# Gathering experts' rows for 144 instead of 128 tokens, and dense products over 368 tokens instead of 384

## The chip, the core and the metric

The kernel runs on one core of one Trainium2 chip. The engines that matter here: TensorE (PE) does the matrix products, VectorE (DVE) and ScalarE (ACT) the elementwise work, GpSimd (POOL) some elementwise work and the issue of indirect DMAs, SyncE (SP) the issue of the weight loads. The metric is device time in microseconds (us), lower is better: the median of several runs of the whole program, which is one launch.

## What is computed

Two transformer blocks in float32, one after the other, on 512 tokens of width 1024 (the second block adds 16 meta tokens). The change touches one layer of the first block, a mixture of 16384 experts, each of them one row of `peer_u` and one row of `peer_v`. Each token picks 16 experts in each of 8 heads:

```python
def peer_ffn(h, w_pq, subkeys, u, v):
    ...
    fin_s, fin_pos = lax.top_k(cand_s, PEER_TOPK)
    expert_idx = jnp.take_along_axis(cand_i, fin_pos, axis=-1)
    gates = jax.nn.softmax(fin_s, axis=-1).astype(h.dtype)
    ...
        u_sel = jnp.take(u, ec, axis=0)
        act = jax.nn.gelu(jnp.einsum('chkd,cd->chk', u_sel, hc), approximate=False) * gc
        v_sel = jnp.take(v, ec, axis=0)
        return jnp.einsum('chk,chkd->cd', act, v_sel)
```

So a token's result is a sum of 128 rows of `v`, each weighted by a gate and by the GELU of a dot product of the token with a row of `u`. The rest of both blocks (convolutions, attention, retention, feed-forward layers) is the same before and after.

## The kernel before

**Two ways through the expert layer.** The last `ND = S - NS` = 384 tokens go the dense way: all 16384 experts are evaluated with matrix products, and a gate matrix that is zero nearly everywhere does the choosing. The first `NS` = 128 tokens go the gathered way, one token per partition: a "row step" fetches for each of the 128 partitions one row of `u` (or of `v`) by an indirect DMA of 512 KB, and VectorE multiplies and sums it. 128 row steps with `u` and then 128 with `v` make up the gathered part (class `_Gathered`; `read` issues the DMA on GpSimd's queue, `step` does VectorE's work and writes the read for two steps later; the tile `row` has `NROW = 4` buffers, so this read waits for the buffer of the step two before).

**The dense way.** Weights come in blocks of 1 MB. Each block is split into a rounded part `whi` (ScalarE, line 95) and a remainder `wlo` (line 96, VectorE in this layer), and each product is three passes: `whi` with both parts of the input and `wlo` with one. A block is 2 column groups x 8 slices of the contraction x 3 passes = 48 matmuls of 128x384 (`mm`, line 184). Experts are taken in 16 groups. A `u` group is 4 `u` blocks (`u_block`: product, GELU, tile `a`), a `v` group 4 `v` blocks that add into `X` (line 1133).

- First stretch: the `u` blocks of the first 12 groups, 48 blocks. Their activations `a` are spilled to DRAM (`ad`). Meanwhile the choice of experts runs on VectorE, and for each dense token two one-hot matrices are made by GpSimd, VectorE and ScalarE (`four`, four tokens at a time) and multiplied on TensorE (`gather`, line 1058) to the gate matrix, which goes to DRAM (`gd`).
- Second stretch: 80 blocks in the order u12, v12, v0, v1, v2, u13, v13, v3, v4, v5, and so on to v11. For a spilled group its gates (`g`, 1.5 MB) and activations (`a`, four pieces of 384 KB) are reloaded on GpSimd's queue during the `v` group ahead of it (`reload`, `back`), multiplied and split on VectorE and ScalarE (`weigh`, lines 1096 and 272 to 274). The tile `g8` has one buffer and `a` three, so the fourth piece of `a` waits until the first has been used. 12 `v` groups have such a reload in them; three (v2, v5, v8) are followed by a `u` group instead, and the last has neither reload nor row steps.

**What sets the order.** Everything that is not a dense product is put on a list `bg` with a cost by hand. After each slice of a product (3 matmuls) `step` adds `rate * t / 512` to a budget and takes items from the list while the budget is positive:

```python
        self.bg_left += self.rate * share
        while self.bg and self.bg_left > 0:
            cost, fn = self.bg.pop(0)
            self.bg_left -= cost
            fn()
```

A row step costs 1.3, a `weigh` 2.1. `EARLY` says how many row steps are woven into each third of the first stretch; `PACE` how many are put on the list per block in the second: `PACE[0]` in a `u` block, `PACE[1]` in a `v` block of a group with a reload (one more at its first block), `PACE[2]` in one of the three groups without. The list sets the order in which instructions are written; each engine then runs its own in that order, and waits for the others by semaphores. Whatever is left on the list at the end of the first stretch is written out at once (`flush`), as are the row steps left at the end (`finish`).

Of the kernel before, what the change touches and what calls it, by code (L numbers as in the profile page):

```python
# [18 lines left out]
P = 128  # L19
D = 1024  # L20
S = 512
NM = 16
T2 = S + NM
KT = D // P
# [6 lines left out]
NS = 128  # L31
ND = S - NS
TCH = 16
# [3 lines left out]
EARLY = (30, 30, 38)  # L37
PACE = (2.4, 1.45, 3.4)
# [756 lines left out]
class _Gathered:  # L795


    def __init__(self, K, tp, H):
        self.K, self.tp, self.H = K, tp, H
# [3 lines left out]
    def rows_of_h(self):  # L803

        nc = self.K.nc
        box = self.K.tp.tile([P, T2], F32, name="acc", tag="acc", bufs=1)
        self.gate, self.dots, self.index = box[:, :P], box[:, P:2 * P], box[:, 2 * P:3 * P].bitcast(U32)
        o = self.K.ps.tile([P, 1024], F32, name="mm", tag="mm", bufs=3)
        for k in range(KT):
            for i in range(2):  # L810
                nc.tensor.matmul(o[:, k * P:(k + 1) * P], self.H[i][:, k, :NS].bitcast(F32), self.K.ident, start=i == 0, stop=i == 1)
        nc.scalar.activation(self.h, o, AF.Copy)

    def begin(self, i, j):
        self.K.nc.vector.scalar_tensor_tensor(self.index, i, float(P), j, op0=OP.mult, op1=OP.add)  # L815
        for _ in range(NROW - 2):
            self.read()

    def read(self):
        n = self.nread  # L820
        if n == 2 * P:
            return
        t = self.tp.tile([P, D], F32, name="row", tag="row", bufs=NROW)
        src = self.K.d["u_rows"] if n < P else self.K.d["v_rows"]
        self.K.nc.gpsimd.indirect_dma_start(out=t, out_offset=None, in_=src,  # L825
                                            in_offset=bass.IndirectOffsetOnAxis(ap=self.index[:, n % P:n % P + 1], axis=0))
        self.rows[n] = t
        self.nread += 1

    def step(self):  # L830
        n, nc = self.ndone, self.K.nc
        s = n % P
        self.ndone += 1
        t = self.rows.pop(n)
        if n < P:
            nc.vector.tensor_tensor_reduce(t, t, self.h, 1.0, 0.0, OP.mult, OP.add, self.dots[:, s:s + 1])  # L836
            if s == P - 1:
                nc.scalar.activation(self.dots, self.dots, AF.Gelu)
                nc.vector.tensor_mul(self.dots, self.dots, self.gate)
        elif s == 0:  # L840
            self.sum = self.tp.tile([P, D], F32, name="sum", tag="hrow")
            nc.vector.tensor_scalar(self.sum, t, self.dots[:, :1], None, op0=OP.mult)
        else:
            nc.vector.scalar_tensor_tensor(self.sum, t, self.dots[:, s:s + 1], self.sum, op0=OP.mult, op1=OP.add)  # L844
        self.read()

# [11 lines left out]
    def more(self, n):  # L858
        self.due += n
        while self.due >= 1 and self.planned < 2 * P:  # L860
            self.K.bg.append((1.3, self.step))
            self.planned += 1
            self.due -= 1

    def finish(self, X):
        K, nc = self.K, self.K.nc
        self.more(2 * P)
        K.flush()
        for i in range(2):
            a = K.aux().rearrange("p (k t) -> p k t", k=4)  # L870
            for k in range(4):
                nc.tensor.transpose(a[:, k], self.sum[:, (4 * i + k) * P:(4 * i + k + 1) * P], K.ident)
            x = X[:, 4 * i:4 * i + 4, :NS]
            nc.vector.tensor_add(x, x, a)


def _peer(K, XA, X, nx):
# [5 lines left out]
    with tc.tile_pool(name="peer", bufs=1) as tp:  # L883
        H = nx.H
        HR = [x[:, :, NS:] for x in H]
        rest = _Gathered(K, tp, H)
# [10 lines left out]
        with tc.tile_pool(name="route", bufs=1) as rp:  # L897
# [78 lines left out]
            def small(name, dt=F32, tag=None):  # L976
                return rp.tile([P, HD * 16], dt, name=name, tag=tag or name, bufs=1)

            def gates(t):
                f = box["v"]  # L980
                v = rest.gate.rearrange("p (h k) -> p h k", h=HD) if t == 0 else rp.tile([P, HD, 16], F32, name="ge", bufs=1)
# [40 lines left out]
            def turn(t):  # L1022
                a = K.aux()
                for n, x in enumerate((box[0], box[1], box["v"].rearrange("p h k -> p (h k)"))):
                    nc.tensor.transpose(a[:, n * P:(n + 1) * P], x, K.ident)
                for n in range(3):
                    nc.vector.tensor_copy(IT[n][:, t * P - NS:(t + 1) * P - NS], a[:, n * P:(n + 1) * P])
                nc.vector.tensor_scalar(IT[3][:, t * P - NS:(t + 1) * P - NS], a[:, :P], -1.0, None, op0=OP.mult)

# [38 lines left out]
            for t in range(1, 4):  # L1068
                K.bg.append((1.8, lambda t=t: turn(t)))
                fours = [(1.1, lambda tb=tb, q=q: four(tb, q))  # L1070
                         for tb in range((t * P - NS) // TCH, ((t + 1) * P - NS) // TCH) for q in range(TCH // 4)]
# [4 lines left out]
            K.rate, K.fine, K.late = 0.64, True, True  # L1076
# [8 lines left out]
        with tc.tile_pool(name="peerv", bufs=1) as vp:  # L1085
# [59 lines left out]
            for n, (kind, g) in enumerate(order):  # L1145
                if n == len(order) - 1:
                    rest.finish(X)
# [699 lines left out]
```

## Time and profile before

| | before |
|---|---|
| median of 3 runs | 3711.65 us (3703.98 to 3716.35) |
| the profiled execution | 3718.03 us |
| its span, first to last instruction | 3716.3 us |
| mean granted clock of TensorE, share of full | 0.983 |
| PE busy in the span | 97% |
| DVE busy in the span | 63% |
| first stretch (48 `u` blocks), from the span's start | 764 to 1304.7 us |
| second stretch, its blocks with row steps | 1304.7 to 1988.5 us |
| second stretch, last 4 blocks | 1988.5 to 2023.3 us |

A busy TensorE is not one at its peak: matmuls overlap, so the busy share hides how far apart they start. The number of matmuls that start in a stretch says that better.

### The profile page before, as it was taken

How to read it: one execution, taken by the hardware profiler on the slowest of the kernel's cores; microseconds unless marked ns; L12 is line 12 of the kernel's file. 1: busy time of each engine (PE TensorE's matmuls, PEld its weight loads, DVE VectorE, ACT ScalarE, POOL GpSimd, SP SyncE). 2: the span in 40 equal slices, each digit the busy share in tenths (PEclk: the TensorE clock that was granted, in tenths of full speed). 3: DMA queues.
4: the chain of work that ended last, by engine and by line, in shares of the span. 5: the costliest groups of instructions: out<-in, count | busy, mean ns of one | idle time of the engine just before them, and what ended most of it. 6: DMA issues, size and time to landing. Idle time of an engine off the chain costs nothing. (4 is left out here: it accounts for less than half of the span.)

```text
span 3716.3 us, 51006 instructions
## 1 busy us (share of the span) xinstructions
PE 3596.8 (97%) x20457; PEld 3269.4 (88%) x20457; DVE 2323.2 (63%) x4126; ACT 1422.8 (38%) x2306; POOL 1179.2 (32%) x940
## 2 busy tenths in 40 slices
PE   8999999998999999999999999989999999999998
PEld 6888788898999899989999999978898889888887
DVE  7896734698888868877887433457534254563334
ACT  4223434235677733323234222333333355442223
POOL 1002323304899934343530100032334333301001
PEclk9999999999999999999999999999999999999999
DMA  3223222236899988888884222231222221332221
GB/s 140 91 102 131 97 102 80 93 118 212 290 298 313 345 302 325 308 293 291 309 320 162 91 91 91 63 111 47 72 83 83 100 88 66 120 111 91 92 101 57
DMA packets 155261, 583.37 MB, mean 157 GB/s; under 512 B 12704, under 2 KB 64032, under 8 KB 112912
## 3 DMA queue, kind: packets, MB, share of 16 engines
q1 hardware_dynamic: 51456, 345.21, 26.5%
q0 software_dynamic: 46576, 190.34, 14.2%
q10 hardware_dynamic: 56992, 44.57, 3.7%
q8 instruction: 161, 2.64, 0.3%
q14 instruction: 76, 0.62, 0.1%
HBM read 527.63 MB, written 52.43 MB: 156 GB/s over the span
## 5 line engine op out<-in xcount | busy, mean ns | idle before, releaser
L184 PE MATMUL mm<-h,whi 128*128 128x512 f32 (+2 forms) x6944 | 1796.4, 351 | 14.4 <-ACT h L380 7.3
L184 PEld LDWEIGHTS mm<-h,whi 128*128 128x128 f32 x6944 | 1195.9, 190 | 146.5 <-ACT h L380 7.3
L184 PE MATMUL mm<-h,wlo 128*128 128x512 f32 (+2 forms) x3472 | 1134.7, 350 | 18.3 <-DVE wlo L96 17.3
L95 ACT ACTIVATE whi<-wraw 128x512 fp32r<-128x512 f32 (+2 forms) x648 | 654.6, 1041 | 524.9 <-PE mm L184 261.2
L184 PEld LDWEIGHTS mm<-h,wlo 128*128 128x128 f32 x3472 | 626.1, 190 | 89.7 <-DVE wlo L96 21.3
L96 DVE TENSOR_TENSOR wlo<-wraw,whi 128x512 fp32r<-128x512 f32 (+2 forms) x387 | 563.5, 1461 | 211.5 <-ACT whi L95 210.9
L96 POOL TENSOR_TENSOR wlo<-wraw,whi 128x512 fp32r<-128x512 f32 (+1 forms) x261 | 436.9, 1696 | 800.7 <-ACT whi L95 765.1
L184 PE MATMUL mm<-w,whi 128*128 128x384 f32 x2048 | 530.4, 340 | 1.4 <-ACT whi L95 1.2
L184 PEld LDWEIGHTS mm<-w,whi 128*128 128x128 f32 x2048 | 376.7, 190 | 2.6 <-ACT whi L95 1.9
L184 PE MATMUL mm<-w,wlo 128*128 128x384 f32 x1024 | 349.5, 341 | 21.0 <-DVE wlo L96 21.0
L1223 POOL TENSOR_TENSOR sl<-sl,r 128x528 f32<-128x528 f32 (+1 forms) x44 | 57.2, 1314 | 732.8 <-ACT sl L1221 732.8
L1037 POOL TENSOR_SCALAR p<-iota,it 128x128 f32<-128x128 f32 x256 | 253.1, 1000 | 44.5 <-ACT whi L95 31.9
L825 POOL DMA_INDIRECT row<-v_rows,acc x128 | 193.1, 1509 | 209.0 <-DVE sum L844 173.5
L184 PE MATMUL mm<-g,whi 128*128 128x264 f32 (+2 forms) x1080 | 226.4, 318 | 0.0
L825 POOL DMA_INDIRECT row<-u_rows,acc x128 | 164.2, 1283 | 176.7 <-DVE acc L815 108.2
L184 PEld LDWEIGHTS mm<-w,wlo 128*128 128x128 f32 x1024 | 194.9, 190 | 25.2 <-DVE wlo L96 25.2
L198 PE MATMUL mm<-whi,h 128*128 128x256 f32 x960 | 181.7, 285 | 7.4 <-DVE tmp L1261 2.6
L844 DVE SCALAR_TENSOR_TENSOR sum<-row,acc,sum 128x1024 f32<-128x1024 f32 x127 | 162.9, 1282 | 33.3 <-DMA row<-v_rows,acc 31.2
L184 PEld LDWEIGHTS mm<-g,whi 128*128 128x128 f32 x1080 | 166.8, 188 | 15.0
L836 DVE CUSTOM_DVE_ANT_0 row<-row,hrow 128x1024 f32<-128x1024 f32 x128 | 156.8, 1232 | 28.2 <-DMA row<-u_rows,acc 28.0
L272 ACT ACTIVATE w<-a 128x384 fp32r<-128x384 f32 x128 | 63.6, 526 | 262.9 <-DVE a L1096 259.2
L198 PEld LDWEIGHTS mm<-whi,h 128*128 128x128 f32 x960 | 151.7, 190 | 9.9 <-DVE v L1295 2.9
(376 smaller groups left out, 4414.5 us busy)
## 6 DMA issues: line engine op xcount, KB each, us to landing
wraw<-uT SPq DMA_DIRECT2D x64, 1024.0 KB, 6.9
wraw<-v SPq DMA_DIRECT2D x64, 1024.0 KB, 7.3
wraw<-w_in SPq DMA_DIRECT2D x27, 1024.0 KB, 4.8
gd<-gc ACTq DMA_DIRECT2D x24, 1024.0 KB, 10.0
g<-gd POOLq DMA_DIRECT2D x16, 1536.0 KB, 8.9
wraw<-ffn_w_gate SPq DMA_DIRECT2D x22, 1024.0 KB, 4.7
wraw<-ffn_w_up SPq DMA_DIRECT2D x22, 1024.0 KB, 4.7
ad<-a ACTq DMA_DIRECT2D x48, 384.0 KB, 7.1
```

The costliest lines, as they stand in the source:

```text
L95: self.nc.scalar.activation(hi[:, a:a + m], t[:, a:a + m], AF.Copy)
L96: eng.tensor_sub(lo[:, a:a + m], t[:, a:a + m], hi[:, a:a + m].bitcast(F32))
L184: self.nc.tensor.matmul(o, a[:, k, (c0 + c) * P:(c0 + c + 1) * P], b[:, k0 + k, lo:hi], start=first and k == 0 and i == 0, stop=last and k ...
L198: self.nc.tensor.matmul(out, x, y, start=start and i == 0, stop=stop and i == 2)
L272: self.nc.scalar.activation(dst[0], src, AF.Copy)
L825: self.K.nc.gpsimd.indirect_dma_start(out=t, out_offset=None, in_=src, in_offset=bass.IndirectOffsetOnAxis(ap=self.index[:, n % P:n % P + ...
L836: nc.vector.tensor_tensor_reduce(t, t, self.h, 1.0, 0.0, OP.mult, OP.add, self.dots[:, s:s + 1])
L844: nc.vector.scalar_tensor_tensor(self.sum, t, self.dots[:, s:s + 1], self.sum, op0=OP.mult, op1=OP.add)
L1037: eng.tensor_scalar(p2[:, j], IOTA, IT[1][:, t:t + 1], None, op0=OP.is_equal)
L1223: nc.gpsimd.tensor_mul(sl[c], sl[c], R)
```

## The change

`NS` goes from 128 to 144. The dense way now covers 368 tokens, so each of its matmuls, and each elementwise operation on its results, is 368 columns wide; the gate matrix is built for 92 instead of 96 groups of four tokens. The 16 tokens that are new on the gathered way are laid out as one head of one token per partition, so 16 row steps with `u` and 16 with `v` are added (`SLOTS` = 16). For them the tokens' vectors are copied eight times over the partitions (`rows_of_h(1)`: four ScalarE copies, 16 products with the identity, one ScalarE copy to a new `hrow`), their indices and gates go through DRAM to that layout (`begin_rest`, four DMAs on GpSimd's queue), and their sums over the heads are formed by a product with a 0/1 matrix `group` in `finish`. The sum of the first 128 tokens is now added to `X` in a step of its own (`fold`) when their last `v` row is done. `EARLY`, `PACE` and the rate of the first stretch are set anew.

```diff
-NS = 128
+NS = 144
+NX = NS - 128
+SLOTS = 8 * 16 * NX // 128
...
-EARLY = (30, 30, 38)
-PACE = (2.4, 1.45, 3.4)
+EARLY = (30, 30, 40)
+PACE = (2.6, 1.85, 3.8)
...
+        self.jobs = [("u", 0, s) for s in range(P)] + [("u", 1, s) for s in range(SLOTS)]
+        self.jobs += [("v", 0, s) for s in range(P)] + [("v", 1, s) for s in range(SLOTS)]
...
+        for k0 in range(0, KT, 4):
+            x = [h[:, k0:k0 + 4, :P].bitcast(F32) for h in self.H]
+            if part:
+                for i in range(2):
+                    x[i] = K.temp().rearrange("p (k t) -> p k t", k=4)
+                    nc.scalar.activation(x[i].rearrange("p k (t h) -> p k t h", t=NX),
+                                         self.H[i][:, k0:k0 + 4, P:NS].bitcast(F32).unsqueeze(3).to_broadcast([P, 4, NX, P // NX]), AF.Copy)
+            for k in range(4):
+                for i in range(2):
+                    nc.tensor.matmul(o[:, (k0 + k) * P:(k0 + k + 1) * P], x[i][:, k], K.ident, start=i == 0, stop=i == 1)
         nc.scalar.activation(self.h, o, AF.Copy)
...
+    def begin_rest(self, i, j, v, t):
+
+        nc = self.K.nc
+        d = self.K.dr.tile([2, NX, P], F32, name="rest")
+        nc.vector.scalar_tensor_tensor(t, i, float(P), j, op0=OP.mult, op1=OP.add)
+        nc.gpsimd.dma_start(d[0], t[:NX].bitcast(F32))
+        nc.gpsimd.dma_start(d[1], v[:NX])
+        for n, x in enumerate((self.index[1].bitcast(F32), self.gate[1])):
+            nc.gpsimd.dma_start(x, d[n].rearrange("t (h k) -> (t h) k", k=SLOTS))
...
+        if last and part == 0:
+            self.K.bg[:0] = [(0.3, lambda: self.rows_of_h(1))] if kind == "u" else [(2.0, lambda: None), (0.5, self.fold)]
...
+    def finish(self):
+        K, nc = self.K, self.K.nc
+        self.more(len(self.jobs))
+        K.flush()
+        a = K.aux()[:, :KT * NX].rearrange("p (k t) -> p k t", k=KT)
+        for k in range(KT):
+            nc.tensor.matmul(a[:, k], self.sum[:, k * P:(k + 1) * P], self.group, start=True, stop=True)
+        x = self.X[:, :, P:NS]
+        nc.vector.tensor_add(x, x, a)
...
-            K.rate, K.fine, K.late = 0.64, True, True
+            K.rate, K.fine, K.late = 0.66, True, True
```

The change moves VectorE's row steps against the reloads. First VectorE in group v15, from its first block to the first `weigh` of the reload written there. Names: `a<-a,g` and `w<-a,w` are a `weigh`, `X<-X,mm` the sum of a `v` block, `wlo` the split of a weight block, `sum<-row,acc,sum` a row step with `v`. The reload itself is written just ahead of the first `X<-X,mm`. Before:

```order
L844 SCALAR_TENSOR_TENSOR sum<-row,acc,sum 128x1024 x2
L1133 TENSOR_TENSOR X<-X,mm 128x384 x2
L96 TENSOR_TENSOR wlo<-wraw,whi 128x2048
L1096 TENSOR_TENSOR a<-a,g_15665 128x384 x2
L274 TENSOR_TENSOR w_11126<-a,w_11125 128x384 x2
```

The same place after the change:

```order
L875 SCALAR_TENSOR_TENSOR sum<-row,acc,sum 128x1024 x3
L1179 TENSOR_TENSOR X<-X,mm 128x368 x2
L98 TENSOR_TENSOR wlo<-wraw,whi 128x2048
L1142 TENSOR_TENSOR a<-a,g_15716 128x368 x2
L276 TENSOR_TENSOR w_11067<-a,w_11066 128x368 x2
```

Three row steps now stand at the head of the group, where two stood. Over the 12 groups with a reload, two steps stood there six times (v0, v1, v13, v7, v15, v9) and three six times (v12, v3, v4, v14, v6, v10); after the change two stand there twice (v4, v14), three nine times, and v9 is a case of its own, shown below.

GpSimd's queue from that reload to the one in v10 (`g<-gd` and `a<-ad` are a reload, `row<-v_rows` the reads of row steps), before:

```order
L1090 DMA g_15665<-gd 128x3072
L1107 DMA a<-ad_4463 128x768 x4
L825 DMA row<-v_rows,acc 128x1024 x7
L1090 DMA g_15948<-gd 128x3072
L1107 DMA a<-ad_4464 128x768 x4
```

And after:

```order
L1136 DMA g_15716<-gd 128x2944
L1153 DMA a<-ad_4463 128x736 x4
L854 DMA row<-v_rows,acc 128x1024 x9
L1136 DMA g_16054<-gd 128x2944
L1153 DMA a<-ad_4464 128x736 x4
```

Nine row reads stand between these two reloads, where seven stood, and all of them still stand behind the four pieces of `a`.

The case of its own is group v9, where the new `fold` falls (`X<-X,aux` is the fold, the line below it the first step of the second sum). VectorE there, after the change:

```order
L875 SCALAR_TENSOR_TENSOR sum<-row,acc,sum 128x1024
L906 TENSOR_TENSOR X<-X,aux 128x4x128 x2
L873 TENSOR_SCALAR sum<-row,acc 128x1024
L1179 TENSOR_TENSOR X<-X,mm 128x368 x2
L98 TENSOR_TENSOR wlo<-wraw,whi 128x2048
L875 SCALAR_TENSOR_TENSOR sum<-row,acc,sum 128x1024
L1142 TENSOR_TENSOR a<-a,g_16054 128x368 x2
```

This reload is written behind the last row step of this piece, so nothing stands on VectorE between it and the `weigh` that needs it; before, a sum and a split stood between them.

## Rows read from the trace of the kernel before

**Rows 1.** The page: busy time of each engine, share of the span, instructions.

```profile
PE 3596.8 (97%) x20457; PEld 3269.4 (88%) x20457; DVE 2323.2 (63%) x4126; ACT 1422.8 (38%) x2306; POOL 1179.2 (32%) x940
```

**Rows 2.** Busy time by stretch (x instructions), granted clock, DMA share, GB/s.

```profile
764.00:887.00 123.00, 113.37 (x657) 110.96 (x656) 116.66 (x447) 49.87 (x88) 2.44 (x2) 0.99 0.40 138
887.00:1280.60 393.60, 386.19 (x2411) 382.11 (x2410) 331.83 (x818) 284.88 (x669) 355.61 (x337) 0.99 0.91 306
1280.60:1304.70 24.10, 17.11 (x99) 15.81 (x97) 18.19 (x44) 14.14 (x35) 19.36 (x18) 0.88 0.99 345
1304.70:1988.50 683.80, 655.49 (x3659) 649.12 (x3658) 545.15 (x637) 218.10 (x236) 268.61 (x220) 0.98 0.83 303
1988.50:2023.30 34.80, 33.78 (x195) 33.45 (x194) 24.37 (x34) 19.82 (x25) 0.00 (x0) 1.00 0.30 111
```

**Rows 3.** The same view: a stretch of 128x384 matmuls, one of 128x264 matmuls.

```profile
1382.20:1482.80 100.60, 100.60 (x578) 100.60 (x577) 83.95 (x111) 31.98 (x31) 46.54 (x37) 1.00 0.89 328
2100.00:2200.00 100.00, 100.00 (x823) 100.00 (x822) 35.84 (x32) 22.51 (x18) 5.30 (x4) 1.00 0.25 85
```

**Rows 4.** Groups by line and shape on TensorE, whole span: small products.

```profile
L1058 PE MATMUL aux<-p,p 128*128 128x128 f32 x768 | 109.4, 282 | 14.4 <-issue 7.8 <-DVE p L1042 3.1 <-POOL p L1037 3.1
...
L811 PE MATMUL mm<-ident,h 128*128 128x128 f32 x32 | 3.7, 275 | 0.0
```

**Rows 5.** Groups on GpSimd, first stretch (764 to 1304.7).

```profile
L1037 POOL TENSOR_SCALAR p<-iota,it 128x128 f32<-128x128 f32 x256 | 253.1, 1000 | 44.5 <-ACT whi L95 31.9 <-DVE it L1027 7.2 <-PE aux L1058 2.0
L825 POOL DMA_INDIRECT row<-u_rows,acc x100 | 124.3, 1243 | 133.3 <-DVE acc L815 108.2 <-issue 11.3 <-DVE acc L836 8.5
```

**Rows 6.** Groups on VectorE, second stretch (1304.7 to 2023.3).

```profile
L96 DVE TENSOR_TENSOR wlo<-wraw,whi 128x2048 fp32r<-128x2048 f32 x80 | 183.1, 2289 | 42.5 <-ACT whi L95 42.4
L844 DVE SCALAR_TENSOR_TENSOR sum<-row,acc,sum 128x1024 f32<-128x1024 f32 x127 | 162.9, 1282 | 33.3 <-DMA row<-v_rows,acc 31.2
L274 DVE TENSOR_TENSOR w<-a,w 128x384 fp32r<-128x384 f32 x128 | 66.1, 557 | 11.8 <-ACT w L272 5.9
L1096 DVE TENSOR_TENSOR a<-a,g 128x384 f32<-128x384 f32 x128 | 65.4, 553 | 54.0 <-DMA a<-ad 54.0
L1133 DVE TENSOR_TENSOR X<-X,mm 128x384 f32<-128x384 f32 x126 | 63.8, 548 | 1.2 <-PE mm L184 1.1
```

**Rows 7.** VectorE's waits, second stretch: us in total, times, longest.

```profile
DVE a L1096 <- DMA a<-ad: 54.0, 11, 7.3
DVE wlo L96 <- ACT whi L95: 42.4, 38, 4.9
DVE sum L844 <- DMA row<-v_rows,acc: 31.2, 13, 5.9
DVE row L836 <- DMA row<-u_rows,acc: 5.5, 3, 3.7
```

**Rows 8.** TensorE's waits, second stretch.

```profile
PE mm L184 <- DVE wlo L96: 27.9, 16, 3.1
```

**Rows 9.** Timeline of VectorE at five of the reloads: start, us, idle before.

```profile
1364.92 1.03 DVE L1096 TENSOR_TENSOR a<-a,g 128x384 f32<-128x384 f32 x2 [7.28 <-DMA a<-ad]
...
1397.31 1.03 DVE L1096 TENSOR_TENSOR a<-a,g 128x384 f32<-128x384 f32 x2 [2.43 <-DMA a<-ad]
...
1608.85 1.03 DVE L1096 TENSOR_TENSOR a<-a,g 128x384 f32<-128x384 f32 x2 [7.08 <-DMA a<-ad]
...
1935.88 1.03 DVE L1096 TENSOR_TENSOR a<-a,g 128x384 f32<-128x384 f32 x2 [3.67 <-DMA a<-ad]
...
1973.02 1.03 DVE L1096 TENSOR_TENSOR a<-a,g 128x384 f32<-128x384 f32 x2 [7.02 <-DMA a<-ad]
```

**Rows 10.** Timeline of GpSimd at two of these reloads.

```profile
1384.16 0.58 POOL L1090 DMA_DIRECT2D g<-gd  x1
...
1598.13 0.58 POOL L1090 DMA_DIRECT2D g<-gd  x1
1598.69 1.67 POOL L1107 DMA_DIRECT2D a<-ad  x3
...
1613.91 0.54 POOL L1107 DMA_DIRECT2D a<-ad  x1 [13.54 <-DVE X L1133]
```

More of the change, by code (lines that the diff above doesn't have):

```diff
@@ L795, with __init__ @@
 class _Gathered:
-    def __init__(self, K, tp, H):
-        self.K, self.tp, self.H = K, tp, H
+    def __init__(self, K, tp, H, X):
+        self.K, self.tp, self.H, self.X = K, tp, H, X
         self.h = tp.tile([P, D], F32, name="hrow", tag="hrow")
         self.rows, self.nread, self.ndone, self.planned, self.due = {}, 0, 0, 0, 0.0
[L803 to L811, printed above, removed]
+        self.jobs = [("u", 0, s) for s in range(P)] + [("u", 1, s) for s in range(SLOTS)]
+        self.jobs += [("v", 0, s) for s in range(P)] + [("v", 1, s) for s in range(SLOTS)]
@@ new lines, in rows_of_h @@
+    def rows_of_h(self, part=0):
+        nc, K = self.K.nc, self.K
+        if part == 0:
+            box = K.tp.tile([P, T2], F32, name="acc", tag="acc", bufs=1)
+            cut = [0, P, 2 * P, 3 * P] + [3 * P + i * SLOTS for i in (1, 2, 3)]
+            a = [box[:, x:y] for x, y in zip(cut, cut[1:])]
+            self.gate, self.dots, self.index = (a[0], a[3]), (a[1], a[4]), (a[2].bitcast(U32), a[5].bitcast(U32))
+            self.group = K.tp.tile([P, NX], F32, name="group")
+            nc.vector.tensor_reduce(self.group, K.ident.rearrange("p (t h) -> p t h", t=NX), AX.X, OP.add)
+        else:
+            self.h = self.tp.tile([P, D], F32, name="hrow", tag="hrow")
+        o = K.ps.tile([P, 1024], F32, name="mm", tag="mm", bufs=3)
+        for k0 in range(0, KT, 4):
[8 more added lines that the diff above has]
+                    nc.tensor.matmul(o[:, (k0 + k) * P:(k0 + k + 1) * P], x[i][:, k], K.ident, start=i == 0, stop=i == 1)
@@ L819, in read @@
     def read(self):
         n = self.nread
[L821 removed]
+        if n == len(self.jobs):
             return
+        kind, part, s = self.jobs[n]
         t = self.tp.tile([P, D], F32, name="row", tag="row", bufs=NROW)
[L824 to L826 removed]
+        self.K.nc.gpsimd.indirect_dma_start(out=t, out_offset=None, in_=self.K.d[kind + "_rows"],
+                                            in_offset=bass.IndirectOffsetOnAxis(ap=self.index[part][:, s:s + 1], axis=0))
@@ L859, in more @@
         self.due += n
-        while self.due >= 1 and self.planned < 2 * P:
+        while self.due >= 1 and self.planned < len(self.jobs):
             self.K.bg.append((1.3, self.step))
@@ L863, in more, with fold @@
             self.due -= 1
-    def finish(self, X):
+    def fold(self):
         K, nc = self.K, self.K.nc
-        self.more(2 * P)
-        K.flush()
         for i in range(2):
@@ L1070, in _peer @@
                 fours = [(1.1, lambda tb=tb, q=q: four(tb, q))
-                         for tb in range((t * P - NS) // TCH, ((t + 1) * P - NS) // TCH) for q in range(TCH // 4)]
+                         for tb in range(max(t * P - NS, 0) // TCH, ((t + 1) * P - NS) // TCH) for q in range(TCH // 4)]
                 if t < 3:
```

36 lines of the change are left out of this document (21 added, 15 removed).

## The prediction

> **What bounds the kernel now.** I read the page first: TensorE is busy 97% of the span [rows 1]. Such a share is no proof that every column taken from a matmul is a gain, so I went stage by stage through the two stretches that the change touches [rows 2]. A matmul of 384 columns starts every 100.6 / 578 = 0.1740 us where nothing disturbs it, one of 264 every 100 / 823 = 0.1215 us [rows 3]: 0.0525 us for 120 columns, 0.4377 ns a column. The stretch from 1304.7 to 1988.5 us holds 76 blocks of 48 matmuls; at 0.1740 us they take 635 us of its 683.8. So nearly 49 us are lost there. TensorE names VectorE's `wlo` for 27.9 us [rows 8]; after such a gap matmuls also start further apart, at a granted clock of 0.98 in the mean and 0.88 at the end of the first stretch [rows 2].
>
> Next I asked what VectorE does there. It is busy 545.2 of 683.8 us [rows 2], and in the waits the other time has names [rows 7]: 54.0 us for reloaded activations, 31.2 and 5.5 for gathered rows, and 42.4 for ScalarE's conversions. Only the last is slack: that split waits where VectorE is ahead. In an in-order queue the other 90.7 us hold up the `wlo` behind them. So VectorE's queue is held for about 545 + 91 = 636 us, as long as the undisturbed matmuls. Both bind already.
>
> **Where the 54 us come from.** Sorted by the row steps written at the head of the group, the reloads fall into two classes [rows 9]. Behind three steps VectorE waits 7.28 (first) to 7.02 us (last), over six reloads 39.6 us, 6.6 each; behind two it waits 2.43 (first) to 3.67 (last), over five of six 14.4 us in all, one not at all, so 2.4 each. The mechanism is on GpSimd's queue [rows 10]: the reload stands behind the reads of those steps, and the third read needs the buffer of the first of them, which VectorE reaches only behind a sum and a split. From the issue of `g` to the first `weigh` it then takes 1608.85 - 1598.13 = 10.7 us. With two steps the last read needs a buffer freed in the group before, and the reload leaves earlier. And the fourth piece waits 13.5 us at the head of the queue, with all row reads behind it.
>
> **The change, first stretch.** Dense: 48 blocks x 48 x 16 columns x 0.4377 ns = -16.1 us. One-hot products: 32 fewer at 109.4 / 768 = 0.142 us [rows 4], -4.6. Not all of this comes. Until 887 us VectorE is busy 116.7 of 123.0 us [rows 2] with the choice of experts, which keeps its work: of 12 blocks' 4.0 us I count 1. From 887 to 1280.6 GpSimd is busy 355.6 of 393.6 us, 90%; it loses 8 comparisons of 1.00 us and gains two row reads of 1.24 [rows 5] and four small DMAs with a trip through DRAM. Of 16.7 us there I count 8. `flush` gets one group of four more, which GpSimd needs about 3 us for (two comparisons and part of a read): +3. Sum -6. Bounds: -14 (a third of TensorE's 20.7 is lost) and +3 (GpSimd is the bound, and the trip through DRAM delays the first comparisons).
>
> **Second stretch, TensorE.** 76 blocks: -25.5 us; the last four: -1.3, of which I count all, since no row step is left there. Added: `rows_of_h(1)` 32 products for 3.7 us [rows 4], the second fold about 1 us.
>
> **Second stretch, VectorE.** The program has 32 more row steps, two of them in the first stretch. 30 x 1.28 us [rows 6] = +38.4. The narrower operations (`w`, `a`, `X`: 66.1 + 65.4 + 63.8 = 195.3 us [rows 6]) lose at most 16/384 of it, -8. The fold's extra sums: +2. Busy: 545 + 32 = 577. The reloads: the order shows nine behind three steps, two behind two, and v9's with nothing in between, which has to sit out the whole 10.7 us. 9 x 6.6 + 2 x 2.4 + 10.7 = 75 instead of 54, +21. Row waits stay at 37. `rows_of_h(1)`: VectorE needs the new `hrow`, which is four ScalarE copies, the products and one more copy away; estimated from the 3.7 us of products and a conversion ahead of it, +5. Other waits about 6. Total 577 + 75 + 37 + 5 + 6 = 700 us, without any slack, against 683.8. Some slack has to stay (the start of u12, and places where a sum waits for its matmul): of 42.4 us I keep 8. So 708: +24. TensorE needs at least 635 - 25.5 + 4.7 = 614 in the same stretch and is not the bound any more. Lower bound: reload waits do not grow (54), row waits halve (18), no slack stays: 577 + 54 + 18 + 5 + 3 = 657, -27. Upper: 7.3 and 3.7 us per reload (84), row waits 45 (the reads stand in longer lines), `hrow` 10, others 8, slack 16: 740, +56.
>
> Gathered bytes are no free term either: 30 more reads of 0.524 MB are +15.7 MB, narrower reloads -1.8, on 683.8 x 0.303 = 207 MB [rows 2].
>
> **Sum.** -6 + 24 - 1 = +17 us. Against the profiled execution's own time that is 3718.0 + 17 = 3735; that execution lay 6.4 us above the median of the runs, so for the median I say 3711.65 + 17 = 3729, in round terms **3728 us**.
>
> **A rule of the skill.** VectorE's products with two operands in memory and GpSimd's issues are seen together in the trace: a read of `u` rows takes 1243 ns to issue in the first stretch [rows 5]. The Trainium skill (GPSIMD Engine Reference, Specifications) says that GpSimd shares its memory interfaces with VectorE and is slowed by VectorE's instructions with two such inputs; by that, more row steps would lengthen the issues as well, and the sum would be nearer to its upper bound. No row here separates the two, so no term rests on it.
>
> **Rivals.**
> - *The dense saving mostly comes.* VectorE is ahead often enough (42.4 us of slack [rows 7]) to take in the 30 steps, and the reload waits shrink since a busier VectorE comes to them later. Then the second stretch gains some 20 us and the first 6 to 14: about 3685. Against it: five reloads go from two steps to three. It decides this way if the reload waits stay under about 55 us and slack falls to nothing. In its purest form, TensorE alone, it is -16.1 - 4.6 - 25.5 - 1.3 + 4.7 = -43: 3669.
> - *A draw.* VectorE's queue grows by 30 us and uses up all of the slack; the first stretch gives back what is over: 3711 plus or minus 11.
> - *The DMA engines become the bound.* The share is 0.83 at 303 GB/s, which is 365 GB/s at a full share; the end of the first stretch reaches 345 at 0.99 [rows 2]. 207 + 13.9 = 221 MB take 605 us at 365, and 729 at the 303 GB/s of now: +45 in that stretch, with the -6 and -1 of the others some 3750. From a share of 0.89 on it costs nothing. The Trainium skill (DMA: Bandwidth & Descriptors, Where 436 GB/s comes from) gives about 358 GB/s for a core when both cores of a memory domain stream; with that the same bytes take 617 us (an estimate from that page). The trace agrees within 2%.
> - *The columns are not paid for*, because a weight load sets the pace. The two rows of 264 and 384 columns speak against it; it would be the added work alone, some 3760.
>
> **How the numbers follow.** VectorE's queue decides (3712, where the slack takes in what is left, to 3711.65 + 56 - 6 - 1 = 3761): 0.52, of which 0.10 ends within the noise. Most of the saving comes: 0.26 at 3675 to 3705, 0.07 of it too small to see; TensorE alone: 0.10; a draw by other ways: 0.04; DMA-bound 0.07; columns unpaid 0.01. What a measurement can tell from no change is 0.3%, 11 us: below 3700.5 is faster, above 3722.8 slower. Faster 0.19 + 0.10 = 0.29; same 0.10 + 0.07 + 0.04 = 0.21; slower 0.42 + 0.07 + 0.01 = 0.50. For the range I go from 3680, inside the case where the saving comes, to 3758, near the top of VectorE's; below it lies about 0.15 (TensorE alone and a sixth of the case above it), above 0.04.
>
> **What would show it.** Right: matmuls of 368 columns start about 0.167 us apart where undisturbed; the second stretch is 700 us or longer although its matmuls need 614; VectorE's waits for reloaded activations grow to about 75 us, its waits for conversions fall under 15, TensorE's waits for `wlo` rise well over 28; one reload, in v9, waits some 10 us. The first stretch is 2 to 10 us shorter, with a longer gap at its end. Wrong: reload waits of 50 us or less, or a second stretch under 680 us, would mean that VectorE had more room than I count; a DMA share over 0.93 there would make the transfers the cause.

## The result and the profile after

The change takes **3743.49 us** (median of 5 runs, 3739.07 to 3749.66) against 3711.65 us (5 runs, 3702.45 to 3717.81): ratio 1.0089, 95% interval 1.0070 to 1.0108, 32 us slower. The forecast was 3728, slower by 16: the time lies in the range, but the change cost twice what was forecast. The profiled execution took 3739.83 us with a span of 3738.0.

By stretch, as in [rows 2] (busy time with instructions, clock, DMA share, GB/s):

```profile
751.90:874.70 122.80, 111.15 (x657) 108.83 (x656) 117.69 (x450) 49.60 (x89) 3.08 (x2) 0.96 0.39 137
874.70:1271.20 396.50, 373.25 (x2372) 365.02 (x2371) 327.74 (x804) 274.53 (x644) 345.84 (x335) 0.98 0.90 303
1271.20:1293.00 21.80, 17.85 (x104) 16.28 (x104) 17.52 (x44) 15.93 (x39) 17.82 (x17) 0.89 0.97 328
1293.00:2024.40 731.40, 655.12 (x3705) 642.40 (x3705) 580.14 (x690) 220.02 (x244) 328.63 (x252) 0.95 0.84 304
2024.40:2058.40 34.00, 32.76 (x195) 32.14 (x195) 21.40 (x31) 18.80 (x23) 0.00 (x0) 1.00 0.26 93
```

First stretch 541.1 us (forecast -6, came +0.4). Second 731.4 instead of 683.8: +47.6 (forecast +24). Last four blocks -0.8 (forecast -1). That is +47, but the span grew by only 21.7 us: the first 751.9 us took 764.0 before, and what follows 2058.4 us is 13.4 us shorter. The change touches none of that code.

In the second stretch TensorE is as busy as before, 655.1 us against 655.5, although each of its products is 16 columns narrower; its granted clock there is 0.95, where it was 0.98. All of the growth is idle time of TensorE: 76.3 us against 28.3.

VectorE's waits in the second stretch (us, times, longest), for [rows 7], then TensorE's, for [rows 8]:

```profile
DVE a L1142 <- DMA a<-ad: 52.9, 10, 8.2
DVE sum L875 <- DMA row<-v_rows,acc: 28.5, 13, 5.9
DVE wlo L98 <- ACT whi L97: 25.7, 30, 3.5
DVE row L867 <- DMA row<-u_rows,acc: 17.7, 6, 4.6
DVE row L867 <- ACT hrow L831: 8.2, 1, 8.2
DVE X L1179 <- PE mm L186: 5.4, 3, 2.5
...
PE mm L186 <- DVE wlo L98: 52.8, 23, 5.5
PE mm L830 <- ACT tmp L826: 8.1, 1, 8.1
PE mm L186 <- ACT whi L97: 6.9, 5, 3.4
PE aux L904 <- DVE sum L875: 4.1, 1, 4.1
```

Read it against the forecast's list. Busy 580 (577 said). Reloads 52.9, not 75. Rows 46, not 37. The second row layout costs 8 us of VectorE and 8 of TensorE. And VectorE still waits 25.7 us for conversions where 8 were to be left. The forecast took these waits as slack and counted 42.4 us of them, but that figure includes the last four blocks; without them it was 34.1 before, so the wait fell by only 8.

### The profile page after: what moved, and what is told of

Read it like the earlier page. It is cut to its first block, busy times and chain, and to the rows that moved or that the text cites. A ratio compares the mean times of both kernels' runs of the same rounds, so it can differ in the third digit from the quotient of the medians.

```text
span 3738.0 us, 51104 instructions
## 1 busy us (share of the span) xinstructions
PE 3550.8 (95%) x20473; PEld 3234.9 (87%) x20473; DVE 2352.3 (63%) x4162; ACT 1414.1 (38%) x2292; POOL 1227.8 (33%) x968
## 5 line engine op out<-in xcount | busy, mean ns | idle before, releaser
L186 PE MATMUL mm<-h,whi 128*128 128x512 f32 (+2 forms) x6944 | 1769.1, 348 | 19.5 <-ACT h L382 8.9
L186 PE MATMUL mm<-h,wlo 128*128 128x512 f32 (+2 forms) x3472 | 1122.6, 346 | 28.4 <-DVE wlo L98 27.6
L186 PEld LDWEIGHTS mm<-h,wlo 128*128 128x128 f32 x3472 | 627.3, 190 | 93.7 <-DVE wlo L98 32.2
L186 PE MATMUL mm<-w,whi 128*128 128x368 f32 x2048 | 525.4, 338 | 5.9 <-ACT whi L97 3.5
L186 PE MATMUL mm<-w,wlo 128*128 128x368 f32 x1024 | 349.5, 341 | 41.4 <-DVE wlo L98 41.3
L854 POOL DMA_INDIRECT row<-v_rows,acc x144 | 226.3, 1572 | 188.9 <-DVE sum L875 154.7
L854 POOL DMA_INDIRECT row<-u_rows,acc x144 | 185.1, 1285 | 205.5 <-DVE acc L834 107.1
L867 DVE CUSTOM_DVE_ANT_0 row<-row,hrow 128x1024 f32<-128x1024 f32 x144 | 175.9, 1232 | 49.6 <-DMA row<-u_rows,acc 41.3
L875 DVE SCALAR_TENSOR_TENSOR sum<-row,acc,sum 128x1024 f32<-128x1024 f32 x142 | 182.2, 1283 | 31.1 <-DMA row<-v_rows,acc 28.5
L274 ACT ACTIVATE w<-a 128x368 fp32r<-128x368 f32 x128 | 61.7, 512 | 302.1 <-DVE a L1142 294.3
```

What stands on the lines that cost most here:

```text
L186: self.nc.tensor.matmul(o, a[:, k, (c0 + c) * P:(c0 + c + 1) * P], b[:, k0 + k, lo:hi], start=first and k == 0 and i == 0, stop=last and k ...
L274: self.nc.scalar.activation(dst[0], src, AF.Copy)
L875: nc.vector.scalar_tensor_tensor(self.sum, t, dots[:, s:s + 1], self.sum, op0=OP.mult, op1=OP.add)
```

## The experiments

Ratios are to the kernel before in the same series; 0.001 is 3.7 us. Lengths of stretches and waits are from one profiled execution each. "Data waits" are VectorE's waits for reloads and rows in the second stretch: 54.0 + 31.2 + 5.5 = 90.7 us before, 99.1 in the change.

**One part alone.** cols_only, with `EARLY` and `PACE` as before (the lists are given in words):

```
-    self.jobs = u steps 0..127, u steps of the last 16 tokens, v 0..127, v of the last 16
+    self.jobs = u steps 0..127, v 0..127       # NS = 144 stays; no second layout, no early fold
```

> The dense products cover 368 tokens and 92 groups of one-hots are made, as in the change, but the 32 row steps and what goes with them are left out (256 row steps, one folding at the end), so the last 16 tokens get no experts. Both theories ask this to be faster than before: 2048 matmuls of 368 columns instead of 384 are worth about 0.007 us each on TensorE alone (14 us in the second stretch, some 7 in the first), or 43 us in all if the 6 per cent of columns comes off every product of both stretches and nothing else ends last. Theory T (the row steps on VectorE's queue cost the time): -25 to -43 us, ratio 0.988 to 0.993. Rival R (what is fixed costs it: the second row layout, the folding between the blocks, the trip through DRAM): the same -25 to -43. A rival of both, that the columns are not paid because VectorE's split of weights ends last in the blocks: -10 us or less, ratio over 0.997.

3692.60 us, ratio 0.9953 (0.9936 to 0.9969): -18 us, below what both theories asked. The first stretch gained 16.5 us, the second 3.7: there the third theory holds.

```profile
1285.10:1965.20 680.10, 633.31 (x3659) 624.32 (x3658) 540.73 (x641) 215.12 (x236) 275.34 (x221) 0.97 0.83 304
```

The 16.5 us are uncertain: in seven profiles of kernels whose first stretch is that of the kernel before (before, before_reload, steps_only and the four with a pad), it took 531.4 to 544.4 us, so the gain is 7 to 20.

rows_only (`NS = 128`, the 32 steps kept, with the change's `EARLY` and `PACE`) and no_extras (`NS = 144`, the 32 steps on the first tokens' indices, no second layout, no early fold):

> The dense products stay at 384 columns and 96 groups of one-hots, and 32 row steps are added with the pacing of the change; they repeat rows of the first tokens and none of the second layout, the trip through DRAM or the folding between the blocks is there (it leaves out what the 16 tokens would get, and adds the 16 repeated slots twice). Theory T: 32 steps of 1.28 us are 41 us of VectorE and push the reloads, +25 to +45 us, ratio 1.007 to 1.012, and the second stretch grows by that. Rival R: the steps fit in VectorE's waits for the other engines, 0 to +8 us, ratio under 1.002. Rival D (the rows' 16 MB more on the DMA queues): as T, but with waits of VectorE for rows over 60 us in the second stretch, where the kernel before had 37.

> The change with its 368 columns, 92 groups and 288 row steps, but without the second row layout (32 products and 4 widening copies of ScalarE), the trip of indices and gates through DRAM, the group product and the folding between the blocks; the 32 steps read rows of the first tokens (it leaves out what the 16 tokens would get). Against the change itself this is the price of what is fixed. Theory T: little of the +32 us goes away, +10 to +22 us remain on the kernel before. Rival R: all of it goes away, and the columns' saving shows: -10 to -30 us, ratio 0.992 to 0.997.

rows_only: 3762.03 us, 1.0139 (1.0119 to 1.0158), +51 us, second stretch 732.0 us: 1.6 us a step, where the work on VectorE is 1.28. Data waits 112.5 us:

```profile
DVE a L1132 <- DMA a<-ad: 64.5, 11, 8.2
DVE sum L873 <- DMA row<-v_rows,acc: 32.0, 14, 5.9
DVE wlo L98 <- ACT whi L97: 23.6, 25, 4.6
DVE row L865 <- DMA row<-u_rows,acc: 16.0, 8, 5.7
```

Rival R falls. Theory T holds in kind, but the ratio is above its 1.007 to 1.012; of D's sign, row waits over 60, there were 48. no_extras: 3754.58 us, 1.0117 (1.0096 to 1.0137), *slower than the change*, which no theory allowed. Its second stretch was like the change's (733.4 us); what differed was, again, code that neither touches. So this had to be settled first.

**The 64 bytes.** `self.group` lies in the pool of temporaries; the pool opened behind it holds the activations that TensorE reads. The change has this tile; the kernel before, cols_only, rows_only and no_extras do not.

```
+ pad = self.K.tp.tile([P, 16], F32, name="group")    # before_pad: 64 bytes more; before_pad2: [P, 32]
- self.group = K.tp.tile([P, NX], F32, name="group")  # after_nopad: into an unused end of `box`
+ self.group = box[:, 3 * P + 3 * SLOTS:3 * P + 3 * SLOTS + NX]
```

> The kernel before with one addition: a tile of 16 numbers per partition (64 bytes) in the pool of temporaries, filled once by the same small sum over the identity that the change makes for its group product, and used by nothing. It moves the pools opened behind it (the activations that TensorE reads are in the next one) by 64 bytes. In the profiles so far the two kernels with such a tile there (the change, gelu_late) had 512-column matmuls spaced by 0.227 us in the stretches that the change doesn't touch, the four without it 0.231 to 0.233, and those stretches were 20 to 24 us shorter. Theory (place in SBUF): -18 to -26 us, ratio 0.993 to 0.995, matmul spacing 0.227. Rival (chance of the execution): ratio 0.999 to 1.001, spacing 0.231 to 0.233.

> The change with that tile of 64 bytes put into the unused end of the tile that holds gates, dots and indices, so that nothing behind the pool of temporaries is moved; the computation is the same. Theory (place in SBUF): 18 to 26 us slower than the change, +50 to +58 us on the kernel before, ratio 1.0135 to 1.0157, spacing of 512-column matmuls 0.231 to 0.233 us. Rival (chance of the execution): as the change, ratio 1.0075 to 1.0105.

> The kernel before with a pad of 128 bytes per partition instead of 64 in the pool of temporaries, so that what lies behind it is moved by twice as much. Theory 1 (any place other than the old one is faster, or every multiple of 64 bytes is): ratio 0.993 to 0.997, spacing of 512-column matmuls 0.227 us in the first 400 us, as with 64 bytes. Theory 2 (the place matters modulo 128 bytes): back to 1.000, spacing 0.231 to 0.233 us.

before_pad 3691.35 us, 0.9952 (0.9935 to 0.9969); after_nopad 3767.21, 1.0159 (1.0142 to 1.0175); before_pad2 3696.23, 0.9971 (0.9957 to 0.9986). The same 50 us, all 512-column matmuls at full clock, in before, the change, before_pad, after_nopad, before_pad2:

```profile
110.00:160.00 50.00, 50.00 (x216) 40.30 (x215) 42.02 (x54) 15.29 (x15) 0.00 (x0) 1.00 0.23 85
...
110.00:160.00 50.00, 50.00 (x222) 41.44 (x221) 43.62 (x56) 12.49 (x13) 0.00 (x0) 1.00 0.29 103
...
110.00:160.00 50.00, 50.00 (x222) 41.40 (x221) 43.44 (x55) 14.16 (x15) 0.00 (x0) 1.00 0.27 89
...
110.00:160.00 50.00, 50.00 (x216) 40.30 (x215) 42.12 (x53) 14.44 (x15) 0.00 (x0) 1.00 0.24 85
...
110.00:160.00 50.00, 50.00 (x220) 41.05 (x219) 43.19 (x55) 13.18 (x14) 0.00 (x0) 1.00 0.28 93
```

216 matmuls or 222 (0.2315 or 0.2252 us each), and 220 with 128 bytes: the place decides, theory 1. The second stretch of the kernel before with 64 bytes, and of the change without them:

```profile
1296.00:1973.50 677.50, 648.96 (x3659) 644.11 (x3658) 546.34 (x641) 218.11 (x236) 277.08 (x220) 0.98 0.83 307
...
1301.10:2042.10 741.00, 657.59 (x3707) 643.52 (x3706) 581.43 (x692) 219.77 (x244) 320.63 (x251) 0.95 0.82 300
```

So the change's own cost at an equal place is not 32 us but some 59 without the 64 bytes (1.0159 - 1) and 51 with them on both sides (1.0089 - 0.9952), and its side effect gives back 18 to 26. At an equal place the second stretch grew by 57 us (741.0 against 683.8) or 54 (731.4 against 677.5), and not by 47.6. At an equal place no_extras is faster than after_nopad by 0.0042 (some 16 us, with 10 either way): the price of what is fixed.

**What the data waits are.** after_reload and before_reload move the reload ahead of the row steps of its group's first block:

```
-   rest.more(...); K.bg.append((0.0, lambda: reload(spilled)))
+   K.bg.append((0.0, lambda: reload(spilled))); rest.more(...)
```

> The change with one thing moved: the reloads of spilled blocks are issued ahead of the row steps of a group's first block and not behind them, so that on GpSimd's queue they no longer stand behind three row reads that each wait for a step of VectorE. Theory T (VectorE with its waits sets the second stretch, and the reload wait is three steps long because of the queue): each of about eight three-step waits of 5 to 8 us falls by 3 steps of 1.28 us, waits for reloads 53 -> 20 to 28 us, the second stretch 731 -> 700 to 707 us, the time +3 to +8 us on the kernel before, ratio 1.000 to 1.003. Rival W (the stall is given back: the row reads now stand behind 1.5 MB of reload): waits for rows grow by what the reloads lose, the time stays within 6 us of the change, ratio 1.007 to 1.0105. Rival P (TensorE sets the stretch): no change either, with waits of both kinds lower.

> The same move in the kernel before. Theory T: the waits for reloads fall from 54 to some 20 to 28 us; in about half of the groups TensorE sets the pace (33.5 us for its 192 matmuls), so only the groups longer than that gain, -8 to -18 us, ratio 0.995 to 0.998. Rival W: the waits for rows grow by as much, ratio 0.999 to 1.001.

after_reload 3743.66 us, 1.0104 (1.0087 to 1.0121): rival W, to the letter.

```profile
DVE sum L875 <- DMA row<-v_rows,acc: 71.7, 21, 7.4
DVE row L867 <- DMA row<-u_rows,acc: 31.4, 7, 6.0
DVE wlo L98 <- ACT whi L97: 27.3, 32, 3.5
```

No wait for a reload is left, and the row waits went from 46 to 103 us: 103.1 in all, from 99.1. before_reload has 78.6 + 11.5 = 90.1 us in place of 90.7, and was slower, 3729.48 us, 1.0058 (1.0042 to 1.0073), which no theory expected: the waits moved into groups that had run at TensorE's pace (v3: 33.5 -> 37.1 us, with TensorE waiting 3.4 us for `wlo` where it had not waited). My class rule (three steps ahead of a reload cost 6.6 us) told where the wait is charged, not how much waiting there is in all.

after_half (no gates in the 12 reloads, 18.1 MB less; the expectation said 11) and after_sp (same bytes, other queue):

```
-   gt = load_g(g)                      # after_half
+   gt = box["g"]
-   nc.gpsimd.dma_start(a, AD[g][b])    # after_sp, and the same in load_g
+   nc.sync.dma_start(a, AD[g][b])
```

> The change with the 1.5 MB of gates (128 partitions of 11.8 KB) left out of each of the 11 reloads of v groups, so that a reload brings 1.5 MB instead of 3 MB; the gates of an earlier group are used again (it leaves out what the right gates would give). Theory B (the waits of VectorE for reloads and rows, 99 us together in the change, are the time that the bytes take): about half of the reload's share goes, waits for a and rows together 99 -> 60 to 75 us, second stretch 731 -> 700 to 712 us, time +1 to +13 us on the kernel before, ratio 1.000 to 1.0035. Rival Q (the waits come from the queue's order, not from bytes): waits 90 us or more, ratio 1.0065 to 1.0095.

> The change with the reloads issued by SyncE, on the queue of the weights, instead of GpSimd's, on which the row reads stand; all bytes stay. Theory B (bytes): waits for reloads and rows together stay within 10 us of 99 us, time that of the change, ratio 1.0065 to 1.0105. Rival Q (queue order): rows and reloads no longer stand behind each other, the two waits together fall to 45 to 70 us, second stretch below 705 us, ratio below 1.003. A third case: SyncE holds back the weights behind a reload that waits for its buffer, TensorE waits for weights, slower than the change by 10 us or more.

after_half 3697.03 us, 0.9975 (0.9962 to 0.9988), second stretch 682.8, data waits 48.6: more than theory B asked. after_sp 3694.42, 0.9962 (0.9948 to 0.9975), second stretch 687.1, with every byte kept: rival Q. Its waits:

```profile
DVE wlo L98 <- ACT whi L97: 43.9, 33, 17.1
DVE sum L875 <- DMA row<-v_rows,acc: 26.3, 14, 6.1
DVE row L867 <- DMA row<-u_rows,acc: 9.2, 5, 3.9
```

Reloads no longer appear, and rows fell as well. The 17.1 us are SyncE holding weights back behind the first load of gates, which itself waits 13.4 us until the gates are written. So most of the waiting (51 to 64 of 99 us) belonged to one queue that carried 3 MB reloads among reads of 0.5 MB; fewer bytes on it, or another queue for them, do the same.

What on that queue makes the wait is not shown. The prediction had seen one candidate: the fourth piece of `a` stands at the head of GpSimd's queue until its buffer is free, with row reads behind it. GpSimd's waits ahead of it in the second stretch, before (two lines), in the change and in after_half:

```profile
POOL a L1107 <- DVE w L274: 126.2, 11, 13.4
POOL a L1107 <- DVE X L1133: 13.5, 1, 13.5
...
POOL a L1153 <- DVE w L276: 127.7, 12, 16.2
...
POOL a L1153 <- DVE w L276: 90.4, 13, 16.3
```

In after_sp this wait is on SyncE and GpSimd has none. But after_half keeps 90.4 us of it and gains as much, so it is not this wait alone. And after_half leaves out the issues of the gates' loads together with their bytes, so it does not show the bytes alone either. The Trainium skill (DMA: Bandwidth & Descriptors, Issuing engines are not separate DMA queues) says that issuing from several engines only saves time on the sequencer, since all DMAs run on the same 16 engines and interleave. The trace agrees that there was nothing to gain in bandwidth: the bytes are the same, and the rate rose from 304 to 327 GB/s because the stretch got shorter. But the move was worth 47 to 49 us. GpSimd's busy time in the stretch fell by some 37 us (328.6 to 291.8), and its wait ahead of the fourth pieces went; which of the two the gain is, no run separates.

**Is the change better off without the stall?** The same move (reloads of v groups alone on SyncE) in the change, in the kernel before with the pad, and in cols_only with the pad; and in the change with the second layout's products issued five row steps early:

```
+   if (part, s) == (0, P - 5):         # after_sp2_early; only the copy PSUM -> hrow stays behind the last step
+       self.K.bg[:0] = [(0.3, lambda: self.rows_of_h(1))]
```

> As after_sp, but only the reloads of v groups are issued by SyncE; the first load of gates and those ahead of u groups stay with GpSimd. In after_sp ScalarE's conversion of weights was late by 17 us at the start of the stretch and TensorE waited 8.4 us for it, since SyncE held the weights back behind the first load of gates. Expected: that wait goes, second stretch 687 -> 677 to 682 us, 5 to 10 us less than after_sp, ratio 0.9935 to 0.9955. Rival: SyncE's reloads elsewhere hold weights back as much, ratio as after_sp, 0.996.

> The kernel before, with the pad of 64 bytes (so that the place in SBUF is that of the change) and the reloads of v groups issued by SyncE. Theory S (the stall carried the change's cost): the kernel before waited 49 us for reloads, but about half of its groups already ran at TensorE's pace, so it gains 15 to 22 us on before_pad and stands at 3670 to 3678 us, ratio 0.990 to 0.9925, within 0.4 per cent of after_sp2. Rival F (the steps themselves cost it): it gains as much as the change did, 40 to 50 us, ratio 0.982 to 0.985, and after_sp2 stays 30 us or more above it.

> cols_only (368 columns, 92 groups of one-hots, 256 row steps; leaves out what the 16 tokens would get) with the pad of 64 bytes and the reloads of v groups issued by SyncE. If TensorE sets the second stretch once the stall is gone, the columns pay their 15 to 27 us there and some 8 in the first stretch: 25 to 35 us below before_pad_sp2, and below after_sp2 by what the 32 steps still cost. If VectorE still sets it, no more than 12 us below before_pad_sp2.

> after_sp2 with the second row layout's widening copies and products issued five row steps earlier into PSUM, and only the copy to SBUF behind the last step of the first 128 tokens. In after_sp TensorE waited 6.7 us for the copies and VectorE 7.4 us for the layout, in a group of 44.6 us where its neighbours took 32. Theory: both waits fall below 3 us, the group falls by 6 to 12 us, ratio 0.002 to 0.003 below after_sp2. Rival: VectorE has slack elsewhere in that stretch and the gain is below 3 us.

after_sp2 3694.93 us, 0.9962 (0.9948 to 0.9976), is no better than after_sp: the wait of 17.1 us is gone (the longest for a conversion is 4.0), but the waits for rows are 48.2 us and not 35.5. **before_pad_sp2 3654.26 us, 0.9853 (0.9835 to 0.9871)**, is faster than both kernels of this case. That is 37 us below before_pad, more than theory S allows and just under F's 40 to 50, and after_sp2 stays 41 us above it, as F says. cols_pad_sp2 3642.03, 0.9829 (0.9814 to 0.9844): the columns are worth 12 us (9 by the ratios, barely clear of noise). after_sp2_early 3682.23, 0.9940 (0.9925 to 0.9956): 12.7 us less than after_sp2 (8 by the ratios, barely clear of noise), TensorE's wait for the copies 7.1 -> 1.9 us and VectorE's for the layout gone. Second stretch of before_pad_sp2 and of after_sp2:

```profile
1286.50:1940.00 653.50, 641.88 (x3657) 638.27 (x3656) 550.27 (x642) 221.02 (x238) 229.98 (x160) 0.99 0.85 319
...
1296.00:1983.50 687.50, 638.02 (x3706) 629.75 (x3706) 580.97 (x692) 221.72 (x244) 291.89 (x192) 0.97 0.86 324
```

TensorE's busy time is about the same; with the change it stands idle 49 us instead of 12. With the reloads on SyncE's queue the change costs 34 us in this stretch (687.5 against 653.5), where it cost 54 with all on GpSimd's, both at an equal place. By the runs' ratios the whole cost falls from 51 to 40 us. So the shared queue carried a part of the change's cost, some 10 to 20 us, and most of it stays without that queue.

**VectorE's work without bytes.** 32 row steps of the second stretch run their VectorE instruction twice on the same row:

```
+   for _ in range(2 if n >= 98 and n % 5 == 0 else 1):
        nc.vector....                   # the step's instruction
```

> The kernel before, where 32 of the 158 row steps of the second stretch run their VectorE instruction twice on the same row (it changes the result: those rows count twice), so that 41 us of VectorE (32 x 1.28) come in and not a byte. Theory V (VectorE's queue sets the stretch, as the prediction summed it): as rows_only, second stretch +40 to +48 us, ratio 1.011 to 1.0139. Theory D (a row step costs its 0.5 MB on the DMA queues; VectorE waits for data anyway, 91 us in the kernel before, and the work goes into those waits): VectorE's waits for a and rows shrink by 20 us or more, +0 to +15 us, ratio 1.000 to 1.004.

> before_pad_sp2 (reloads issued by SyncE) with the same 32 doubled steps. There VectorE waits only 30 us for rows, and 50 us for ScalarE's conversion, while TensorE works 642 of 653 us. Theory V: +20 to +35 us on before_pad_sp2, ratio 0.991 to 0.995. Theory D: the work goes into the waits, +0 to +12 us, ratio 0.9853 to 0.9885; then the 41 us between after_sp2 and before_pad_sp2 are the bytes' and the fixed extras'.

steps_only 3726.24 us, 1.0056 (1.0037 to 1.0076): +20 us, between the two theories. VectorE's waits:

```profile
DVE a L1098 <- DMA a<-ad: 46.2, 11, 7.1
DVE wlo L96 <- ACT whi L95: 29.0, 29, 4.2
DVE sum L846 <- DMA row<-v_rows,acc: 24.4, 9, 7.6
...
DVE row L837 <- DMA row<-u_rows,acc: 4.6, 2, 3.2
```

VectorE's busy time grew by 41.1 us; data waits fell by 15.5 and conversion waits by 5.1; the stretch grew by 20.2. In rows_only, with the bytes, busy grew by 38.4, conversion waits fell by 10.5, but data waits *grew* by 21.8. So of a step's 1.6 us about 0.6 is VectorE's work. The other 1.0 came with its row, or with the new `EARLY` and `PACE`, which rows_only has and steps_only has not; that it is the row's bytes is argued and not shown. steps_pad_sp2 3670.55 us, 0.9905 (0.9887 to 0.9923): +16 us on before_pad_sp2 (19 by the ratios), between the theories too.

**Two moves without effect.** gelu_late puts the GELU of the first 128 tokens behind the second layout's copies; after_ulate defers the weighing in u groups:

> The change with one thing moved: the GELU and the gate product of the first 128 tokens stand behind the second row layout in ScalarE's and VectorE's queues, so that ScalarE's widening copies no longer wait for VectorE's last row step. In the change's profile TensorE waited 8.1 us there for the copies and VectorE then 8.2 us for the layout. Theory: a wait of 5 to 8 us goes away, and the time is +24 to +28 us on the kernel before, ratio 1.0065 to 1.0075, with TensorE's wait for the copies under 3 us. Rival: the wait only moves to the copy of the layout, which has to wait for the same step, and the time is that of the change, +30 to +34 us.

> The change with one thing moved: in u groups the weighing of blocks 0 and 1 comes among the next block's matmuls instead of just ahead of the next weights' split, so that in 8 of 12 places VectorE's split no longer stands right behind a chain of VectorE, ScalarE (w), VectorE, ScalarE (whi, 2 us). In the change VectorE waits 13.2 us for whi in the four u groups. Theory V (VectorE's busy time and its waits add up to the second stretch): 8 waits of 1.2 us go, VectorE's waits for whi 25.7 -> 16 to 19 us, time 5 to 10 us less than the change, ratio 1.006 to 1.0075. Rival: the waits come back as waits for rows and reloads, which are late anyway, and the time is the change's, ratio 1.008 to 1.0105.

gelu_late 3741.06 us, 1.0083 (1.0068 to 1.0098): TensorE's wait for the copies 8.1 -> 5.6 us, VectorE's came back as 4.5 us for the GELU. after_ulate 3740.29 us, 1.0088 (1.0072 to 1.0105): conversion waits 25.7 -> 24.4, reload waits 52.9 -> 58.2. In time both rivals held. In after_ulate the conversion waits did not come back as other waits; they hardly went.

## Why the prediction was right in sign and short in size

The step that failed is the price of the 30 row steps in the second stretch. The prediction put them at 38.4 us of VectorE's time, left row waits at 37 us without giving a reason, and let all but 8 us of the conversion waits be used up. Measured were row waits of 46.2 us and conversion waits of 25.7, and rows_only took 48 us for these steps in this stretch at 384 columns. Two errors the other way hid part of it: reload waits 22 us too high in the sum, and 18 to 26 us that the change gains by its place in SBUF.

- *Matmuls of 368 columns start 0.167 us apart where undisturbed*: held; in v4, 192 of them took 32.2 us, with the clock at 1.00:

```profile
1608.20:1640.40 32.20, 32.20 (x194) 32.00 (x193) 29.11 (x35) 10.34 (x11) 15.93 (x13) 1.00 0.93 350
```

- *VectorE's queue decides the second stretch, TensorE's 614 us do not*: held as to TensorE: cols_only gained 3.7 us of the 25.5 there. As to VectorE it is half true: 41 us more of its work made the stretch 20 us longer (steps_only).
- *Second stretch +24*: came +47.6; this is the sum that failed. Its terms: busy 577, measured 580.1; reload waits 75, measured 52.9 (v9's was 0.2 and not 10.7; v1, behind three steps, had none and waited 8.2 us for `hrow` instead; the other eight behind three steps had 6.3 each); row waits 37, measured 46.2; `hrow` 5, measured 8.2; other 6, measured 18; slack 8, measured 25.7. The total of the waits, 131, came as 151. The largest miss is "of 42.4 us I keep 8": in the runs that had the 32 steps with their bytes on GpSimd's queue that wait was 6 to 11 us shorter, and in cols_only, without these steps, 9.7, so it is not shown that in the change the steps took it up.
- *v9 sits out the whole reload*: failed. The section on the change says that nothing stands on VectorE between this reload and its `weigh`. GpSimd issued it at 1954.59 us, and before the `weigh` VectorE did most of the fold, two row steps, a sum and a split:

```profile
1954.59 0.58 POOL L1136 DMA_DIRECT2D g<-gd  x1
...
1964.12 0.99 DVE L1142 TENSOR_TENSOR a<-a,g 128x368 f32<-128x368 f32 x2 [0.16 <-DMA a<-ad]
```

- Behind the sum stands one mis-sized price: a row step at 1.28 us of VectorE, with its bytes weighed as a rival and left out of the sum. rows_only measured 1.6 for the whole step, and steps_only 0.6 for VectorE's part. About half of VectorE's work does go into waits, as the first rival had it; with their reads the steps bring new waits (data waits +21.8 us in rows_only, -15.5 in steps_only).
- *Rival "DMA engines become the bound"*: its price (+45 there, 729 us) was met by 731.4, but not by its mechanism; the share was 0.84, and after_sp moved the same bytes in 687 us. The queue that the reads share with the reloads carried a part of the cost; without it 41 us are left.
- *First stretch -6*: came +0.4, within the bounds. One profile cannot tell these apart: kernels with the change's first stretch took 534.6 to 544.6 us in nine profiles, those with the old one 531.4 to 544.4 in seven. no_extras, without the trip through DRAM, has 533.6; that the trip took the saving is not shown.
- *Nothing elsewhere*: wrong by -25.5 us in the profile, -18 to -26 by the paired runs. The pad of `group` was not in the sum. Without it the time would have been 3767 (after_nopad), above the range. That the time lies in the range is luck: this gain, most of it in code that the forecast did not look at, took off part of a cost that was forecast too low.

What stays open: why rows and reloads on GpSimd's queue wait as long as they do (its transfers or its issues); no run took one without the other. Open too is what after_sp2's 41 us over before_pad_sp2 are made of. The narrower columns give back some 12 of what is added, so 53 are to be explained: if the parts add up, 16 are VectorE's work (steps_pad_sp2) and 13 the layout (after_sp2_early), and some 24 are left for the rows' bytes, the fold, the trip through DRAM and the new order. And no run shows why TensorE's granted clock was lower in the change.

## What to carry to other kernels

Where an engine in the chain waits for data, do not price an added step by its instruction alone: here 41 us of VectorE's work made the stretch 20 us longer, and 32 steps with their reads, in a new order, made it 48 us longer. Reordering issues within one queue moved the wait and did not shorten it. Do not count on a wait as slack: of 34 us, 26 stayed. And when a change adds even a small tile, compare stretches that it does not touch.

## What the runs showed of the hardware that was not expected

- 64 bytes more in a pool ahead of the activations changed 512-column matmuls from 216 to 222 in 50 us at a granted clock of 1.00, with the same instructions: 0.5% of the kernel (before_pad), 0.7% back (after_nopad). Which address it is that counts was not tried.
- Moving 3 MB reloads from GpSimd's queue to SyncE's took 37 us off the kernel before (0.9952 to 0.9853, both with the pad) and 47 to 49 off the change, with every byte kept.
